# Token norms one projection earlier, and the first head pair's substitution handed out inside the second pair

## The chip, the cores and the metric

One core of one Trainium2 chip. The time is the device time of one execution in microseconds, the median of three runs. The engines are TensorE (PE, matmuls and transposes), VectorE (DVE), ScalarE (ACT), GpSimd (POOL) and SyncE (SP, which issues most DMAs). Each runs its own queue of instructions in order and waits on semaphores for the others.

## The reference

A decoder layer on 2048 tokens of width 1024, in float32: a gated DeltaNet mixer with 8 heads of 128, then a squared-ReLU MLP of width 4096, each behind an RMS norm and with a residual, and a last RMS norm.

```python
proj = h @ w_in                                   # q, k, v, gate z, and b, a
qkv = silu(causal_depthwise_conv(proj[..., :3 * DN_WIDTH], conv_w))   # 4 taps
...
lower = where(strict, einsum('bhnid,bhnjd->bhnij', k_beta, k) * decay, 0.0)
rhs = concatenate([v * beta, k_beta * exp(gc)])
sol = triangular_solve(lower + eye, rhs, lower=True, unit_diagonal=True)
...
x = x + gated_deltanet(rms_norm(x, norm_mix))
x = x + squared_relu_mlp(rms_norm(x, norm_mlp))
return rms_norm(x, norm_final)
```

The triangular matrix of each chunk of tokens is inverted: the 32x32 blocks on its diagonal by forward substitution, row by row, the rest from these blocks by matmuls.

## The kernel before

**Blocks and halves.** The tokens go in two blocks of 1024. Each block runs its mixer and then its MLP; the two mixers lie at about 0 to 740 and 1440 to 2200 us of the span. A mixer goes through two halves of 512 tokens (s = 0 and 1), and in each through the 8 heads in four pairs.

**A pair** has six projections, in the order k, k, q, q, v, v, counted by `n` from 1 to 6. Each is 24 matmuls of 128x512 (L117 to L119, 8 slices of the width, each as three products of high and low parts) into a PSUM bank `pj`, of which there are three. ACT copies it to `raw` (L303, L304; two buffers), DVE adds the other three taps (three L307), ACT takes a tanh (L310) and DVE finishes the SiLU (L311). After the third and fourth projection stand the key matrices (L428 on PE, L430 and L438 on DVE, with the decay factors `dt` of L413 and L415). In block 0's first half the weights come raw: POOL splits each into two parts (L90, L91) and SP keeps the result in DRAM; later they are read back.

**The substitution** of a pair is the generator `rows_of`: a transpose `pr` (L324), then 31 pairs of a multiply (L332) and a sum (L334) on DVE, in 24 steps. Its result `tt` is transposed at L344 (`tr`), and from there the inverse is built on PE and ACT (L364 to L391). This inverse, transposes of keys and values (L468), and the scores of queries and keys (L477) are the stages of the *previous* pair (`prepare2`), one stage behind each projection of the current pair. `wind_up` then runs the previous pair's two gate projections (L535, L536) and its chain over the chunks (L495 to L514, ending in the output `o`, L529), into which rows of the current pair's substitution are filled. For the first pair of a mixer there is no previous pair, and all its rows are handed out at once behind its projections.

**The norm of the other half.** In the first half (s = 0), each pair also norms one tile of 128 tokens of the second half: a DMA of the tile `xt`, the sum of squares on ACT (L180), a reciprocal root by DVE (L145, L130, L131, three L135 and L139), the scaled tile `xn` (L181), eight transposes on PE (two groups of four L186) and the split into two parts (L189 on ACT, L190 on DVE). The first pair computes the decay gates besides (`gg`, L263, which PE sums up at L268).

**What sets the order.** The program order gives priorities; a scheduler lists each engine's instructions from them once, and each queue then runs in that order whatever comes. `xt`, `xn` and `pr` share four buffers.

Of the kernel before, what the change touches and what calls it, by code (L numbers as in the profile page):

```python
# [7 lines left out]
F32 = mybir.dt.float32  # L8
# [8 lines left out]
P = 128  # L17
D = 1024
# [4 lines left out]
HB = 512  # L23
HT = HB // P
HP = 2
# [8 lines left out]
def tile_kernel(ctx: ExitStack, tc: tile.TileContext, x, w_in, w_out, w_up, w_down, n_mlp, n_fin, consts, out):  # L34
# [3 lines left out]
    pe, act, dve, pool, sp = nc.tensor, nc.scalar, nc.vector, nc.gpsimd, nc.sync  # L38
# [33 lines left out]
    for h in range(NH):  # L72
        s = cp.tile([P, P], F32, name=f"S{h}")
# [47 lines left out]
    def half_tiles():  # L121
        hh = hp.tile([P, KS, HB], F32R, name="hh", tag="hh")
        hl = hp.tile([P, KS, HB], F32R, name="hl", tag="hl")
        return hh, hl
# [52 lines left out]
    def norm_transpose(i, src, xn, wcol, hh, hl, tag):  # L177

        ssq = sm.tile([P, 1], F32, name="ssq", tag="ssq", bufs=3)
        act.activation(xn, src, AF.Square, accum_out=ssq)  # L180
        dve.tensor_scalar_mul(xn, src, rstd_of(ssq))  # L181
        ti = slice(i * P, (i + 1) * P)
        for k4 in range(0, KS, 4):
            ps = big(tag)
            for k in range(4):
                pe.transpose(ps[:, k * P:(k + 1) * P], xn[:, (k4 + k) * P:(k4 + k + 1) * P], ident)  # L186
            for k in range(4):
                src_, w = ps[:, k * P:(k + 1) * P], wcol[:, k4 + k:k4 + k + 1]
                act.activation(hh[:, k4 + k, ti], src_, AF.Copy, scale=w)  # L189
                dve.scalar_tensor_tensor(hl[:, k4 + k, ti], src_, w, hh[:, k4 + k, ti].bitcast(F32),  # L190
                                         op0=MULT, op1=SUB)
            yield
# [389 lines left out]
    def mixer(blk, hT):  # L582
        with tc.tile_pool(name="ap", bufs=2) as ap:
# [27 lines left out]
            def stages_of(sb, h, hT, qkv, gt, u):  # L611
                return prepare2(ap, sb, h, *qkv, gt, u, ub, t64)

            gt = None
            for s in range(2):
                sb = 2 * blk + s
                for h in range(0, NH, HP):
                    qkv, n = [], 0
                    stages = stages_of(*prev) if prev is not None else iter(())
                    next(stages, None)  # L620
                    if s == 0 and h == 0:
                        hT2 = half_tiles()
                    for part in (1, 0, 2):
                        d = ap.tile([P, HP * HB], F32, name=f"c{part}", tag=f"c{part}")
                        qkv.append(d)
                        for j in range(HP):
                            conv_part(ap, hT, part, h + j, d[:, j * HB:(j + 1) * HB], sb)
                            n += 1
                            next(stages, None)
                            if s == 0 and h == 0 and n <= 3:  # L630
                                if n == 1:
                                    gt = {}
                                    g_steps = gates(ap, sb, hT, gt)
                                next(g_steps)


                            if n == 3:
                                u = prepare(ap, sb, h, gt)
                                key_matrices(u, qkv[0], 0)
                            if n == 4:  # L640
                                key_matrices(u, qkv[0], 1)
                                key_norms(u)
                                rows_of = invert_diagonal(ap, u)
                                finish_ready()
                            if blk == 0 and s == 1 and n in (2, 5):
                                split_out(h // HP * 2 + n // 5)
                            if s == 0 and n == 1:
                                xt = wp.tile([P, D], F32, name="xt", tag="xt", bufs=4)
                                r0 = (sb + 1) * HB + h // HP * P
                                sp.dma_start(xt, x[r0:r0 + P, :])  # L650
                            if s == 0 and n == 2:
                                xt_steps = norm_transpose(
                                    h // HP, xt, wp.tile([P, D], F32, name="xn", tag="xt", bufs=4), nmix, *hT2, "po")
                            if s == 0 and n in (2, 4):
                                next(xt_steps)
                            if s == 0 and h == NH - HP and n >= 4:
                                if n == 4:
                                    gt2 = {}
                                    g_steps = gates(ap, sb + 1, hT2, gt2)
                                next(g_steps, None)  # L660
                    if prev is not None:
                        ready += wind_up(stages, rows_of, *prev)
                    for _ in rows_of:
                        pass
                    prev = sb, h, hT, (qkv[1], qkv[0], qkv[2]), gt, u
                if s == 0:
                    for _ in g_steps:
                        pass
                    hT, gt = hT2, gt2
# [224 lines left out]
```

## Time and profile before

| | us |
|---|---|
| median of 3 runs | 2877.57 (2872.32 to 2878.12) |
| the profiled execution | 2877.12 |
| its span | 2875.3 |
| PE busy in the span | 2751.3 |
| DVE busy in the span | 1563.4 |

The span runs from the first to the last instruction; 1.8 us of the profiled execution lie around it. The granted clock of TensorE is 0.98 of full speed over the whole span. In rows of the profile, "x4 [12.84 <-DVE xn L181]" says that four instructions ran, that the engine stood idle for 12.84 us before them, and that DVE's instruction of line 181, which writes `xn`, ended this idle time. In a row of a stretch the engines stand in the order PE, PEld (weight loads), DVE, ACT, POOL, each with its busy time and the number of instructions.

### The profile page before, as it was taken

The page shows a single profiled execution, that of the slowest core. Times are in us where ns is not written, and L with a number is a line of the kernel's source. Part 1 is how long each engine was busy: PE and PEld are TensorE (multiplying, and loading weights), DVE is VectorE, ACT ScalarE, POOL GpSimd, SP SyncE. Part 2 cuts the span into 40 slices and gives each one's busy share as a digit, 9 for nine tenths or more (in the row PEclk, how much of TensorE's full clock was granted, in tenths as well). Part 3 has the DMA queues.
Part 4 walks back from the last instruction along what each step waited for, and adds up shares of the span by engine and source line. Part 5 has one row for each costly group of instructions (what it writes and reads, how often), then busy time and mean ns, then how long its engine had stood idle before and what let it go on. Part 6 is the DMA issues. An engine that isn't in the chain of part 4 may idle for free.

```text
span 2875.3 us, 38577 instructions
## 1 busy us (share of the span) xinstructions
PE 2751.3 (96%) x14584; PEld 2278.5 (79%) x14584; DVE 1563.4 (54%) x3814; ACT 935.7 (33%) x2274; POOL 727.4 (25%) x646
## 2 busy tenths in 40 slices
PE   7788999999999999999999999999899999999998
PEld 6576778877788888888877888887787888888887
DVE  7887777763434333333388776777434333333335
ACT  4343444454221211211245555454423111112112
POOL 5443222210142332322311111111003322322321
PEclk9898999999999999999999999999999999999999
DMA  6544455556521211111144434444472111111111
GB/s 229 194 154 154 169 187 186 183 197 210 186 70 44 59 44 45 59 45 44 59 172 166 154 130 150 146 148 177 154 260 68 58 40 50 52 39 57 52 37 66
DMA packets 77482, 337.52 MB, mean 117 GB/s; under 512 B 8560, under 2 KB 8816, under 8 KB 55792
## 3 DMA queue, kind: packets, MB, share of 16 engines
q1 hardware_dynamic: 58480, 292.98, 30.3%
q10 hardware_dynamic: 18816, 42.08, 4.3%
q8 instruction: 114, 1.87, 0.3%
q14 instruction: 72, 0.59, 0.1%
HBM read 271.98 MB, written 63.05 MB: 117 GB/s over the span
## 4 chain that ended last, share of the span: by engine, by line
PE 79%; DVE 13%; ACT 5%; issue 2%; DMA 1%; POOL 1%; ACTq 0%; POOLq 0%; DVEq 0%; SPq 0%
PE pj L117 13%; PE pj L118 13%; PE pj L119 13%; PE kq L118 8%; PE kq L119 8%; PE kq L117 8%; DVE c L307 3%; DVE tmp L332 2%; PE kq L510 1%; DVE tt L334 1%; PE kq L504 1%; PE po L117 1%; PE po L119 1%; PE kq L495 1%; PE po L118 1%
## 5 line engine op out<-in xcount | busy, mean ns | idle before, releaser
L117 PE MATMUL pj<-hh,w 128*128 128x512 f32 x2048 | 819.6, 400 | 0.0
L118 PE MATMUL pj<-hh,w 128*128 128x512 f32 x2048 | 816.2, 399 | 0.0
L119 PE MATMUL pj<-hl,w 128*128 128x512 f32 x2048 | 814.1, 398 | 0.0
L119 PEld LDWEIGHTS pj<-hl,w 128*128 128x128 f32 x2048 | 389.6, 190 | 79.5 <-issue 0.6
L118 PEld LDWEIGHTS pj<-hh,w 128*128 128x128 f32 x2048 | 390.9, 191 | 76.7
L117 PEld LDWEIGHTS pj<-hh,w 128*128 128x128 f32 x2048 | 390.4, 191 | 76.8 <-issue 0.4
L739 ACT ACTIVATE r<-pj 128x512 f32<-128x512 f32 x128 | 76.6, 599 | 1066.0 <-PE pj L119 1066.0
L742 DVE TENSOR_TENSOR ul<-r,uh 128x512 fp32r<-128x512 f32 x128 | 146.8, 1147 | 485.6 <-ACT uh L741 485.6
L119 PE MATMUL kq<-dl,uh 128*128 128x512 f32 x992 | 386.9, 390 | 0.0
L118 PE MATMUL kq<-dh,ul 128*128 128x512 f32 x992 | 386.8, 390 | 0.0
L117 PE MATMUL kq<-dh,uh 128*128 128x512 f32 x992 | 386.7, 390 | 0.0
L782 DVE TENSOR_TENSOR x<-kq,x 128x512 f32<-128x512 f32 x256 | 176.6, 691 | 202.1 <-PE kq L119 199.4
L307 DVE SCALAR_TENSOR_TENSOR c<-raw,cst,c 128x512 f32<-128x512 f32 x288 | 246.4, 860 | 61.2 <-ACT c L304 58.6
L90 POOL TENSOR_SCALAR w<-wr 128x1024 fp32r<-128x1024 f32 x106 | 114.1, 1077 | 599.2 <-PE po L119 309.2
L782 DVE TENSOR_TENSOR x1h<-kq,x1h 128x512 f32<-128x512 f32 x256 | 176.5, 691 | 155.8 <-PE kq L119 155.6
L91 POOL TENSOR_TENSOR w<-wr,w 128x1024 fp32r<-128x1024 f32 x106 | 258.1, 2435 | 6.8
L90 POOL TENSOR_SCALAR dh<-wr 128x1024 fp32r<-128x1024 f32 x62 | 63.9, 1046 | 659.2 <-PE kq L118 626.4
L117 PEld LDWEIGHTS kq<-dh,uh 128*128 128x128 f32 x992 | 186.3, 188 | 40.3 <-DVE rm L145 1.4
L118 PEld LDWEIGHTS kq<-dh,ul 128*128 128x128 f32 x992 | 186.2, 188 | 39.4
L119 PEld LDWEIGHTS kq<-dl,uh 128*128 128x128 f32 x992 | 186.2, 188 | 38.8
L332 DVE TENSOR_TENSOR tmp<-tt,pr 128x2 f32<-128x2 f32 (+30 forms) x496 | 161.7, 326 | 10.3 <-POOL pr L325 0.5
L91 POOL TENSOR_TENSOR dl<-wr,dh 128x1024 fp32r<-128x1024 f32 x62 | 147.3, 2394 | 0.5
(313 smaller groups left out, 3432.7 us busy)
## 6 DMA issues: line engine op xcount, KB each, us to landing
w<-wi SPq DMA_DIRECT2D x96, 1024.0 KB, 4.9
wi<-w SPq DMA_DIRECT2D x32, 1024.0 KB, 4.8
wr<-in_w_up SPq DMA_DIRECT2D x64, 512.0 KB, 3.6
w<-wo SPq DMA_DIRECT2D x32, 1024.0 KB, 5.6
wr<-in_w_down SPq DMA_DIRECT2D x64, 512.0 KB, 3.5
wr<-in_w_in SPq DMA_DIRECT2D x32, 512.0 KB, 5.7
qe<-eg_d ACTq DMA_DIRECT2D x16, 512.0 KB, 3.8
o_d<-z2s ACTq DMA_DIRECT2D x32, 256.0 KB, 2.7
```

The lines of the kernel that those rows point to most:

```text
L90: pool.tensor_scalar(dst_h, src, 1.0, 0.0, op0=MULT, op1=ADD)
L91: pool.tensor_tensor(dst_l, src, dst_h.bitcast(F32), op=SUB)
L117: pe.matmul(ps, ah, bh, start=first and i == 0, stop=False)
L118: pe.matmul(ps, al, bh, start=False, stop=False)
L119: pe.matmul(ps, ah, bl, start=False, stop=last and i == n - 1)
L307: dve.scalar_tensor_tensor(dst, raw[:, k:k + HB], cw[:, 4 * f + k:4 * f + k + 1], dst, op0=MULT, op1=ADD)
L332: dve.tensor_tensor(tmp[:, 0:n, 0:i + 1], tt[:, 0:n, 0:i + 1], pr[:, i, 0:i + 1].unsqueeze(1).to_broadcast([P, n, i + 1]), op=MULT)
L334: dve.tensor_reduce(tt[:, 0:n, i], tmp[:, 0:n, 0:i + 1], axis=mybir.AxisListType.X, op=ADD)
L495: pe.matmul(ps[:, 0:P], u["k2"][:, c * P:(c + 1) * P], st[j], start=True, stop=True)
L739: act.activation(r, ps, AF.Relu)
L742: dve.tensor_tensor(ul[:, hs], r, uh[:, hs].bitcast(F32), op=SUB)
L782: dve.tensor_tensor(dst, ps, dst, op=ADD)
```

## The change

Two things change in both mixers, and all later lines of the program move on (L181 becomes L182, L186 L187, L344 L345, L364 L365, L468 L469).

1. The norm's generator yields once more, behind `xn`. The tile's DMA now stands ahead of the pair's first projection; the norm up to `xn` comes behind the first projection (n = 1), the two groups of transposes behind the second and the fourth. Before, the DMA stood behind the first projection, the norm and the first transposes behind the second.
2. The first pair's rows are no longer handed out at once. Behind the second pair's first projection come 12 of its steps, behind the second the other 12; the stages of the first pair start only then, and the last of them run in `wind_up` between the gate projections.

```diff
         dve.tensor_scalar_mul(xn, src, rstd_of(ssq))
+        yield
...
-                    next(stages, None)
-                    if s == 0 and h == 0:
-                        hT2 = half_tiles()
+                    late = s == 0 and h == HP
+                    if not late:
+                        next(stages, None)
+                    if s == 0:
+                        xt = wp.tile([P, D], F32, name="xt", tag="xt", bufs=4)
+                        r0 = (sb + 1) * HB + h // HP * P
+                        sp.dma_start(xt, x[r0:r0 + P, :])
+                        xt_steps = norm_transpose(
+                            h // HP, xt, wp.tile([P, D], F32, name="xn", tag="xt", bufs=4), nmix, *hT2, "po")
                     for part in (1, 0, 2):
...
                             n += 1
-                            next(stages, None)
+                            if s == 0 and n in (1, 2, 4):
+                                next(xt_steps)
+                            if late and n < 3:
+                                for _ in range(12 * n):
+                                    next(rows_of, None)
+                            if not late or n > 1:
+                                next(stages, None)
...
-                            if s == 0 and n in (2, 4):
-                                next(xt_steps)
...
-                    for _ in rows_of:
-                        pass
+                    if prev is not None:
+                        for _ in rows_of:
+                            pass
```

What this does to the queues shows at three places, all in block 0, first half. On TensorE, the start of the first pair's inverse (L364, now L365). Before, it stands in the middle of the second pair's last projection (w_1197, values), behind transposes of the first pair (c_606 its values, c_261 its keys):

```order
L117 MATMUL pj<-hh,w_1197 128x512
L118 MATMUL pj<-hh,w_1197 128x512
L468 MATMUL po<-cst,c_606 128x128 x4
L468 MATMUL po<-cst,c_261 128x128 x3
L364 MATMUL kq<-tcm,mt 32x32 x8
L468 MATMUL po<-cst,c_261 128x128
L119 MATMUL pj<-hl,w_1197 128x512
```

Now it stands in the projection behind that one (w_1206, the first gate), with the second pair's key products (c_692) next to it:

```order
L117 MATMUL pj<-hh,w_1206 128x512
L118 MATMUL pj<-hh,w_1206 128x512
L365 MATMUL kq<-tcm,mt 32x32 x8
L429 MATMUL kq<-c_692 128x128 x4
L119 MATMUL pj<-hl,w_1206 128x512
```

The inverse has moved behind 30 more dense matmuls, and the 16 transposes, eleven of which stood ahead of it, all follow it now.

On DVE, the second pair's scaled tile. Before, it stands among the later rows of the first pair's substitution, between two convolutions of the second pair's keys (c_774):

```order
L139 SCALAR_TENSOR_TENSOR rst<-rt,rst 128x1
L311 SCALAR_TENSOR_TENSOR c_774<-raw,c_774 128x512
L332 TENSOR_TENSOR tmp<-tt,pr 128x5x17
L181 TENSOR_SCALAR xn<-xt,rst 128x1024
L334 TENSOR_REDUCE tt<-tmp 128x5
L332 TENSOR_TENSOR tmp<-tt,pr 128x5x18
```

Now both pairs' scaled tiles (the second L181 below is the second pair's) stand around the very first convolution of the mixer (c_264, the first pair's keys):

```order
L181 TENSOR_SCALAR xn<-xt,rst 128x1024
L139 SCALAR_TENSOR_TENSOR rst<-rt,rst 128x1
L135 TENSOR_SCALAR rt<-rst,rh 128x1
L139 SCALAR_TENSOR_TENSOR rst<-rt,rst 128x1
L135 TENSOR_SCALAR rt<-rst,rh 128x1
L139 SCALAR_TENSOR_TENSOR rst<-rt,rst 128x1
L308 SCALAR_TENSOR_TENSOR c_264<-raw,cst,c_264 128x512
L181 TENSOR_SCALAR xn<-xt,rst 128x1024
L308 SCALAR_TENSOR_TENSOR c_264<-raw,cst,c_264 128x512 x2
```

The tile no longer waits for rows of the substitution.

On DVE, the end of the first pair's substitution. Before, it comes behind the first tap of the second pair's values (c_1110):

```order
L332 TENSOR_TENSOR tmp<-tt,pr 128x256
L307 SCALAR_TENSOR_TENSOR c_1110<-raw,cst,c_1110 128x512
L334 TENSOR_REDUCE tt<-tmp 128x8
L190 SCALAR_TENSOR_TENSOR hl<-po,cst,hh 128x128
L344 STREAM_TRANSPOSE tr<-tt 128x256
L307 SCALAR_TENSOR_TENSOR c_1110<-raw,cst,c_1110 128x512
```

Now the first head's values are done and two taps of the second head's as well (c_1089 holds both):

```order
L333 TENSOR_TENSOR tmp<-tt,pr 128x8x31
L312 SCALAR_TENSOR_TENSOR c_1089<-raw,c_1089 128x512
L335 TENSOR_REDUCE tt<-tmp 128x8
L333 TENSOR_TENSOR tmp<-tt,pr 128x256
L308 SCALAR_TENSOR_TENSOR c_1089<-raw,cst,c_1089 128x512
L335 TENSOR_REDUCE tt<-tmp 128x8
L308 SCALAR_TENSOR_TENSOR c_1089<-raw,cst,c_1089 128x512
L345 STREAM_TRANSPOSE tr<-tt 128x256
```

Five convolution instructions more stand ahead of the transpose. In block 1 the same places move likewise: the inverse stands behind 22 more dense matmuls, `xn` of the second pair among the gates' instructions ahead of `gg`, with three L307 (now L308) and an L311 of the queries ahead of `gg` too.

More of the change, by code (lines that the diff above doesn't have):

```diff
@@ L612, in stages_of @@
                 return prepare2(ap, sb, h, *qkv, gt, u, ub, t64)
-            gt = None
+            gt, hT2 = None, half_tiles()
             for s in range(2):
@@ L646, in mixer @@
                                 split_out(h // HP * 2 + n // 5)
[L647 to L653, printed above, removed]
-                            if s == 0 and n in (2, 4):
-                                next(xt_steps)
                             if s == 0 and h == NH - HP and n >= 4:
```

## The prediction

> **What bounds the kernel now.** I read the page first, then what TensorE waits for in the two mixers, then the stretches around those waits on TensorE and on DVE. From the page:
>
> ```profile
> span 2875.3 us, 38577 instructions
> PE 2751.3 (96%) x14584; PEld 2278.5 (79%) x14584; DVE 1563.4 (54%) x3814; ACT 935.7 (33%) x2274; POOL 727.4 (25%) x646
> PE 79%; DVE 13%; ACT 5%; issue 2%; DMA 1%; POOL 1%; ACTq 0%; POOLq 0%; DVEq 0%; SPq 0%
> ```
>
> TensorE is busy 96% of the span, so an edit that removes no matmul can win only its idle time and its slow time. DVE holds 13% of the chain though it is busy for half the span: somewhere DVE is the bound. The waits of TensorE, first in block 0's mixer (0 to 900 us), then in block 1's (1440 to 2200 us), with total, count and longest:
>
> ```profile
> PE po L186 <- ACT o L529: 12.9, 2, 7.7
> PE po L186 <- DVE xn L181: 12.8, 1, 12.8
> PE po L468 <- ACT vt L471: 7.4, 2, 5.2
> PE po L268 <- DVE gg L263: 4.5, 1, 4.5
> ...
> PE po L186 <- DVE xn L181: 5.8, 1, 5.8
> ```
>
> The change moves two things that stand here: the wait for the scaled token tile (L181, 12.8 and 5.8 us, one per block, both in the second head pair), and the place of the first pair's substitution. Around the larger wait TensorE reads:
>
> ```profile
> 93.24 1.11 PE L186 MATMUL po<-cst,xn 128*128 128x128 f32 x4 [12.84 <-DVE xn L181]
> ...
> 94.58 0.63 PE L119 MATMUL pj<-hl,w 128*128 128x512 f32 x1
> ...
> 98.84 0.53 PE L117 MATMUL pj<-hh,w 128*128 128x512 f32 x1
> ```
>
> From 94.58 to 98.84 lie ten dense matmuls, 0.43 us apart. What they take in a stretch where TensorE is never idle, and how the engines share the time around the wait, stands in the windows:
>
> ```profile
> 740.00:1440.00 700.00, 697.53 (x3089) 576.29 (x3089) 252.67 (x354) 131.91 (x223) 220.08 (x128) 1.00 0.19 60
> ...
> 57.00:122.30 65.30, 46.78 (x202) 37.89 (x200) 63.59 (x135) 26.32 (x62) 40.22 (x36) 0.87 0.56 198
> 122.30:150.00 27.70, 27.40 (x220) 22.77 (x220) 14.58 (x54) 16.35 (x38) 10.87 (x11) 0.86 0.43 147
> 150.00:187.00 37.00, 27.45 (x155) 23.69 (x155) 34.49 (x104) 10.61 (x37) 15.24 (x11) 0.92 0.43 147
> ```
>
> The columns are TensorE, weight loads, DVE, ACT, POOL, then the granted clock. In the MLP a matmul takes 697.53 / 3089 = 0.226 us, so the ten lost 4.26 - 2.26 = 2.0 us after the wait. From 57 to 122.3 us DVE is busy 63.59 of 65.30 us while TensorE has 18.5 us to spare: **here DVE is the bound, and the 12.84 us are only where that shows.** From 122.3 to 150 us it is TensorE (27.40 of 27.70), and from 150 DVE again. The border is the end of the first substitution:
>
> ```profile
> 120.71 1.11 PE L468 MATMUL po<-cst,c 128*128 128x128 f32 x4 [5.21 <-ACT vt L471]
> ...
> 122.33 0.43 DVE L344 STREAM_TRANSPOSE tr<-tt 128x256 f32<-128x256 f32 x1
> ...
> 123.50 1.06 PE L364 MATMUL kq<-tcm,mt 32*32 32x32 f32 x16
> ```
>
> L344 ends the substitution, and the inverse on TensorE starts with L364, 1.2 us behind.
>
> **The change, part by part.** Work is neither added nor removed; the sum is of places in the queues.
>
> *The second pair's norm, block 0.* It leaves the DVE stretch 57 to 122.3 us and goes in front of the first convolutions. What that stretch holds:
>
> ```profile
> L307 DVE SCALAR_TENSOR_TENSOR c<-raw,cst,c 128x512 f32<-128x512 f32 x22 | 27.0, 1228 | 0.2 <-ACT c L304 0.2
> L139 DVE SCALAR_TENSOR_TENSOR rst<-rt,rst 128x1 f32<-128x1 f32 x3 | 2.6, 877 | 0.0
> L135 DVE TENSOR_SCALAR rt<-rst,rh 128x1 f32<-128x1 f32 x3 | 0.8, 271 | 0.0
> L181 DVE TENSOR_SCALAR xn<-xt,rst 128x1024 f32<-128x1024 f32 x1 | 0.7, 747 | 0.0
> ...
> 85.88 2.33 DVE L139 SCALAR_TENSOR_TENSOR rst<-rt,rst 128x1 f32<-128x1 f32 x1
> ...
> 90.15 0.74 DVE L307 SCALAR_TENSOR_TENSOR c<-raw,cst,c 128x512 f32<-128x512 f32 x1
> ```
>
> The norm is 0.8 + 0.7 + 2.6 = 4.1 us, of which one L139 of 2.33 us was held by something that will hold another instruction instead: I take **-2.0** (bounds -4.1 and 0, the latter if the head has no room for it).
>
> *The substitution, block 0.* In the new order the last row and L344 stand behind five more convolution instructions of the pair's values: 5 x 0.74 = **+3.7**. The 22 L307 took 27.0 us instead of 22 x 0.74 = 16.3. The excess of 10.7 us lies beside POOL's splits of the weights:
>
> ```profile
> L91 POOL TENSOR_TENSOR w<-wr,w 128x1024 fp32r<-128x1024 f32 x8 | 20.3, 2539 | 0.2
> ...
> 94.35 2.88 POOL L91 TENSOR_TENSOR w<-wr,w 128x1024 fp32r<-128x1024 f32 x1
> ...
> 95.08 2.70 DVE L307 SCALAR_TENSOR_TENSOR c<-raw,cst,c 128x512 f32<-128x512 f32 x1
> ```
>
> Eight splits, 1.3 us of hold each. TensorE, no longer stopped at 80 us, frees weight buffers earlier, so one or two more splits (the gate projections') fall before L344: I take one, **+1.3** (0 to 2 x 2.0, the 2.70 row less 0.74). The Trainium skill ("SBUF — State Buffer", "Who interferes with whom") says that a DVE instruction with two SBUF inputs and a GpSimd instruction reading SBUF exclude each other for a whole instruction; the 2.70 us row beside the 2.88 us one agrees, and by it an extra split could cost its full 2.5 us, the sum then 1.2 us worse.
>
> *The gates, block 0.* DVE reaches gg some 1 us later (two more L307 and three more L430 ahead of it, but a shorter run of gate rows), while TensorE has 10 more dense matmuls in front of L268:
>
> ```profile
> 48.90 0.61 PE L268 MATMUL po<-gg,cst 128*128 128x32 f32 x2 [4.48 <-DVE gg L263]
> ...
> 51.02 0.63 PE L117 MATMUL pj<-hh,w 128*128 128x512 f32 x1
> ...
> 54.43 0.55 PE L119 MATMUL pj<-hl,w 128*128 128x512 f32 x1
> ...
> 57.30 0.29 DVE L430 SCALAR_TENSOR_TENSOR mt<-kq,cst 128x128 f32<-128x128 f32 x1 [3.58 <-PE kq L428]
> ```
>
> 10 x 0.226 = 2.3 less 1.0 is 1.3; eight steps from 51.02 to 54.43 took 3.4 instead of 1.8 us, and a shorter idle may save part of that. DVE waits for this at 57.30, so it counts: **-2.0** (-3 to +2).
>
> So L344 moves by -2.0 + 3.7 + 1.3 - 2.0 = **+1.0 us**, to about 123.3. TensorE, without the 12.84 us, reaches the inverse at about 107 us and waits there instead. What it has gained by then is order: 30 dense matmuls that stood behind L364 now stand ahead of it (6.8 us), and 11 of the 16 L468 transposes that stood ahead now follow (11 x 0.28 = 3.1 us by the 1.11 us row of four). From 122.3 to 150 us TensorE has 3.7 us less to do, and it is the bound there. Net in block 0: -3.7 + 1.0 = **-2.7 us** (-9 to +5).
>
> *Block 1.* The rows:
>
> ```profile
> 1543.45 1.12 PE L186 MATMUL po<-cst,xn 128*128 128x128 f32 x4 [5.80 <-DVE xn L181]
> ...
> 1565.48 0.69 PE L364 MATMUL kq<-tcm,mt 32*32 32x32 f32 x16 [0.20 <-ACT tcm L346]
> ...
> 1508.45 0.18 DVE L263 TENSOR_TENSOR gg<-gg,nexpa 128x32 f32<-128x32 f32 x1
> ...
> 1526.83 1.25 DVE L324 STREAM_TRANSPOSE pr<-xc 128x1024 f32<-128x1024 f32 x1 [0.99 <-ACT xc L322]
> ```
>
> The 5.80 us go, with about 0.6 us of slow matmuls behind them. TensorE comes to L364 with 22 more dense matmuls done (5.0 us), so 1.4 us sooner than now, when it waited 0.20 us: it will wait for the substitution. Against it, gg now follows three L307, an L311 and the norm's L181, about +4 us on 1508.45; the decay factors follow gg, the matrices them, and L324 them. DVE had about a microsecond of idle before L324, so I let the substitution start 2.5 us later, without the norm in its way (-2.0) but behind three more convolution instructions (+2.1 us): L344 comes +2.6. Net 2.6 - 5.0 = **-2.4 us** (-6.4 to +3).
>
> *The rest, at nothing.* The token tile's DMA stands in front of the pair's first weight on SP, and keep stores and loads of weights come in pairs: a load issued one split later. Its cover in block 0 is the wait at L364, over 12 us; without it a late weight costs up to a split, 2.5 us. The third and fourth pairs keep the order of their substitutions.
>
> Sum: 2877.1 (the profiled execution, 0.4 us below the median; its span is 1.8 us shorter) - 2.7 - 2.4 = 2872.0, or with a quicker inverse, since 30 matmuls fewer stand between its steps, about a microsecond less. I forecast **2871 us**.
>
> **The rivals.** *Both waits vanish whole.* If the DVE rows had room, 12.84 + 2.0 + 5.80 + 0.6 = 21.2 us would go, and the time be about 2856. For it: the two waits are the only ones for L181. Against it: DVE's 63.59 of 65.30 us. 0.12.
>
> *The waits only change their place.* TensorE stops at the inverse for as long as it stopped for the tile, and starts again at half pace, as it did after 12.84 us (ten steps, 2.0 us lost). L344 then comes 3 to 4 us later, and the 3.7 and 5.0 us of order are used up: 2875 to 2878. For it: DVE is the bound up to L344 and its work is the same. Against it: TensorE is the bound right behind. 0.30. The Trainium skill ("TensorE: Matmul & The Clock Gate", "What's actually happening") has the array at half rate after an idle window of about 3.4 us, until it has been busy about as long. The 12.84 us wait agrees. By that rule a wait of over 3.4 us at the inverse in block 1 costs the half rate that I left out, 1.7 us, and the sum would be 2873: it speaks against the change, which moves long waits rather than ends them.
>
> *Slower: the first substitution ends late.* If each of three further splits holds DVE for 2.0 us (the 2.70 row less 0.74) and the norm's room in front is not there, L344 in block 0 moves by 3.7 + 6.0 + 2.0 = 11.7 instead of 1.0 us; with 3.7 us of order against it, block 0 loses 8.0 us, and with block 1 at nothing the time is 2885. It decides from the point where L344 stands past about 126 us (122.33 + 3.7). For it: the 1228 ns mean of L307; against it: the eight splits there already cost only 1.3 us each. 0.18.
>
> **How the numbers follow.** My forecast has the remaining 0.40. What this kernel's measurement can tell from no change is about 0.2%, 5.8 us: 2871 is 6.6 us under the median, so just beyond. Faster by more than that: 0.31 of the forecast's 0.40 (2865 to 2876), the whole gain's 0.12, and 0.04 of the moved waits, where L344 comes earlier than they say; 0.47. Within: 0.09 of the forecast, 0.25 of the moved waits, 0.02 of the late substitution; 0.36. Slower: 0.16 and 0.01; 0.17. The range reaches from 2857, near the whole gain, to 2884, near the late substitution.
>
> **What would show it.** In the profile after: no wait for L181 in either mixer; the longest wait of the first mixer at the inverse's first matmul, for the copy behind L344, 12 to 18 us long; L344 within 2 us of 123 us; the second pair's transpose L324 (147.32 us now) some 3 us earlier. In block 1 gg near 1512 us and a wait of some 4 us at the inverse.
>
> ```profile
> 147.32 1.25 DVE L324 STREAM_TRANSPOSE pr<-xc 128x1024 f32<-128x1024 f32 x1 [1.87 <-ACT xc L322]
> ```
>
> Wrong would be made by an L344 past 126 us, by a wait for a weight's split in the second pair, or by a longer wait for L529 (12.9 us in two) that gives the 3.7 us back.

## The result, and the profile after

| | median us | runs | ratio to before (95%) |
|---|---|---|---|
| before | 2881.17 (2872.32 to 2889.08) | 20 | |
| changed | 2886.68 (2881.81 to 2890.97) | 20 | 1.0019 (1.0011 to 1.0027) |

Slower by 5.5 us (3.2 to 7.8), where 2871 was forecast, 6.6 us faster than the median of three runs that the forecast was counted from. That median, 2877.57, was 3.6 us under the 2881.17 of these twenty runs of the same kernel. The changed kernel's profiled execution took 2881.81 us, its fastest of the 20, over a span of 2880.0 us. From its page:

```profile
span 2880.0 us, 38585 instructions
PE 2759.5 (96%) x14584; PEld 2285.1 (79%) x14584; DVE 1563.9 (54%) x3814; ACT 936.0 (33%) x2274; POOL 727.3 (25%) x646
PE 75%; DVE 14%; ACT 5%; DMA 2%; issue 2%; POOL 2%; ACTq 0%; SPq 0%; POOLq 0%; DVEq 0%
```

The same 14584 matmuls are busy 8.2 us longer (2759.5 against 2751.3), and TensorE stands idle 3.5 us less (2880.0 - 2759.5 = 120.5 against 124.0). Between these two executions what was lost is not idle time: the matmuls ran slower. The waits of TensorE in block 0's mixer (0 to 900 us), with total, count and longest:

```profile
PE po L187 <- ACT o L530: 10.9, 2, 5.6
...
PE po L269 <- DVE cc L434: 6.1, 1, 6.1
...
PE kq L365 <- ACT tcm L347: 4.7, 2, 4.5
PE po L237 <- ACT kt L472: 4.6, 1, 4.6
PE pj L118 <- POOL w L91: 4.5, 2, 2.4
PE pj L117 <- POOL w L90: 4.4, 2, 2.8
```

and in block 1's (1440 to 2200 us):

```profile
PE kq L365 <- ACT tcm L347: 8.6, 3, 6.1
```

No wait for the scaled tile is left, as the change says. In its place stand four waits for POOL's splits of the weights (L90, L91), 4.5 us at the inverse (L365) and a longer wait at the gates' sum (L269, 6.1 us for 4.5). Where TensorE's time to the inverse went, row by row in block 0 and then at block 1's inverse:

```profile
81.23 0.50 PE L117 MATMUL pj<-hh,w 128*128 128x512 f32 x1 [1.61 <-POOL w L90]
84.11 0.79 PE L118 MATMUL pj<-hh,w 128*128 128x512 f32 x1 [2.38 <-POOL w L91]
...
112.33 0.51 PE L117 MATMUL pj<-hh,w 128*128 128x512 f32 x1 [2.75 <-POOL w L90]
114.94 0.79 PE L118 MATMUL pj<-hh,w 128*128 128x512 f32 x1 [2.10 <-POOL w L91]
115.53 0.63 PE L119 MATMUL pj<-hl,w 128*128 128x512 f32 x1
...
126.22 1.06 PE L365 MATMUL kq<-tcm,mt 32*32 32x32 f32 x16 [4.51 <-ACT tcm L347]
...
1569.60 1.05 PE L365 MATMUL kq<-tcm,mt 32*32 32x32 f32 x16 [6.13 <-ACT tcm L347]
```

Behind each pair of waits for the splits 14 dense matmuls start 0.43 us apart, half the pace of one every 0.226 us: TensorE reaches the inverse at 121.7 us, not 107. DVE's marks, and the stretch that answers to 57 to 122.3 us of before:

```profile
51.00 0.19 DVE L264 TENSOR_TENSOR gg<-gg,nexpa 128x32 f32<-128x32 f32 x1
...
125.05 0.44 DVE L345 STREAM_TRANSPOSE tr<-tt 128x256 f32<-128x256 f32 x1
...
143.06 1.25 DVE L325 STREAM_TRANSPOSE pr<-xc 128x1024 f32<-128x1024 f32 x1 [1.19 <-ACT xc L323]
```

```profile
57.00:125.05 68.05, 55.86 (x221) 44.15 (x219) 63.76 (x130) 24.82 (x57) 41.19 (x37) 0.90 0.57 209
```

DVE is still the bound to the end of the first substitution, with as much work as before (63.76 us against 63.59), and that end comes 2.7 us later (125.05 against 122.33). The second pair's transpose then comes 4.3 us earlier than before (143.06 against 147.32): up to there the forecast's order pays.

To see where a lead is won and lost I compare when TensorE starts the same dense matmul of w_in, counted from the start, as changed minus before: -2.7 us at 205 us, -1.9 at 272 and still at 292, +0.6 at 336, +1.2 at the end of block 0, and +4.7 at the end. Most of the lead goes at 292 to 336 us, in the fourth pair. The change moves the norm of a tile in that pair too, and with it the work around the second half's gates. There TensorE waits for a copy by ACT, before and changed:

```profile
316.44 1.06 PE L236 MATMUL po<-cst,bat 32*128 32x16 f32 x8 [2.83 <-ACT kt L471]
```

```profile
315.28 1.60 PE L237 MATMUL po<-cst,bat 32*128 32x16 f32 x8 [4.62 <-ACT kt L472]
```

From 292 to 331 us the changed kernel loses 2.6 us against before, and so does each of the three further profiles below that have its order there; before's own three further ones lose 0.0 to 1.1. The wait is 4.4 to 4.7 us in all eleven profiles whose block 0 has the moved norm, and 2.8 in all nine that have it as before. The experiments look for the rest: what block 0 loses against other executions of before, and block 1.

### The profile page after: what moved, and what is told of

The parts are those of the page before. It is cut to its first block, busy times and chain, and to the rows that moved or that the text cites. A ratio compares the mean times of both kernels' runs of the same rounds, so it can differ in the third digit from the quotient of the medians.

```text
span 2880.0 us, 38585 instructions
## 1 busy us (share of the span) xinstructions
PE 2759.5 (96%) x14584; PEld 2285.1 (79%) x14584; DVE 1563.9 (54%) x3814; ACT 936.0 (33%) x2274; POOL 727.3 (25%) x646
## 4 chain that ended last, share of the span: by engine, by line
PE 75%; DVE 14%; ACT 5%; DMA 2%; issue 2%; POOL 2%; ACTq 0%; SPq 0%; POOLq 0%; DVEq 0%
PE pj L118 13%; PE pj L117 13%; PE pj L119 13%; PE kq L119 8%; PE kq L118 8%; PE kq L117 8%; DVE c L308 3%; DVE tmp L333 2%; DVE tt L335 1%; PE kq L511 1%; PE kq L505 1%; PE po L117 1%; PE po L119 1%; PE po L118 1%; PE kq L496 1%
## 5 line engine op out<-in xcount | busy, mean ns | idle before, releaser
L117 PE MATMUL pj<-hh,w 128*128 128x512 f32 x2048 | 821.5, 401 | 4.6 <-POOL w L90 4.4
L117 PEld LDWEIGHTS pj<-hh,w 128*128 128x128 f32 x2048 | 391.0, 191 | 82.7 <-POOL w L90 5.0
L117 PE MATMUL kq<-dh,uh 128*128 128x512 f32 x992 | 386.6, 390 | 0.0
L308 DVE SCALAR_TENSOR_TENSOR c<-raw,cst,c 128x512 f32<-128x512 f32 x288 | 245.2, 857 | 61.4 <-ACT c L305 57.6
L91 POOL TENSOR_TENSOR w<-wr,w 128x1024 fp32r<-128x1024 f32 x106 | 258.9, 2443 | 7.0
L90 POOL TENSOR_SCALAR w<-wr 128x1024 fp32r<-128x1024 f32 x106 | 113.9, 1075 | 570.1 <-DMA wr<-in_w_up 210.2
L90 POOL TENSOR_SCALAR dh<-wr 128x1024 fp32r<-128x1024 f32 x62 | 63.9, 1047 | 659.0 <-PE kq L118 626.2
L117 PEld LDWEIGHTS kq<-dh,uh 128*128 128x128 f32 x992 | 186.2, 188 | 40.4 <-DVE rm L145 1.4
L91 POOL TENSOR_TENSOR dl<-wr,dh 128x1024 fp32r<-128x1024 f32 x62 | 147.3, 2394 | 0.5
```

The source lines that it names most:

```text
L90: pool.tensor_scalar(dst_h, src, 1.0, 0.0, op0=MULT, op1=ADD)
L91: pool.tensor_tensor(dst_l, src, dst_h.bitcast(F32), op=SUB)
L117: pe.matmul(ps, ah, bh, start=first and i == 0, stop=False)
L308: dve.scalar_tensor_tensor(dst, raw[:, k:k + HB], cw[:, 4 * f + k:4 * f + k + 1], dst, op0=MULT, op1=ADD)
```

## The experiments

Ratios are to runs of before on the same chip, taken beside each kernel's. Kernels without a ratio ran once.

**Each half of the change alone.** The norm alone undoes the second part of the change, the rows alone the first (both edits shortened):

```diff
-                            if late and n < 3:          # norm alone
-                                for _ in range(12 * n):
-                                    next(rows_of, None)
...
-                            if s == 0 and n in (1, 2, 4):   # rows alone: the norm's steps at n = 2 and 4 again
-                                next(xt_steps)
```

> Only the norm is moved; the first pair's rows are handed out at once as before. In its order gg (the gates' result on DVE) is late as in the changed kernel: 10 dense matmuls more ahead of L269 in each block. Gates theory (the norm step ahead of the gates makes gg, and with it the decay factors and the whole first substitution, late): gg near 1512 to 1515 us in block 1 (1508.45 before), L345 2 to 4 us later than before in both blocks, time 3 to 6 us above before. Weights theory (loads in pairs on SP make TensorE wait for POOL's splits): waits for a split's w of about 9 us in the first mixer again, time 3 to 6 us above before. Rows theory (handing out the rows later is what costs): no slower than before.

> Only the first pair's rows are handed out inside the second pair; norm and tile DMA as before, so gg and the second pair's xn stand where they stood. Gates theory: gg at 48.6 and 1508.4 us as before, waits for xn of about 13 and 6 us as before, time within 2 us of before. Rows theory: time 4 to 6 us above before, with the loss at the inverse L365. Weights theory: no waits for a split's w over 1 us, time as before.

Norm alone: 2874.26 us, 0.9977 (0.9965 to 0.9989): faster by 6.6 us, and by 12 us than both together. Rows alone: 2879.44 us, 0.9988 (0.9973 to 1.0003). Neither half is slow, so the sum of the parts' costs does not explain the whole; something between them does.

**The gates.** The changed order has `gg` 2.4 us later in block 0 and 6.4 us in block 1 (1.2 of them because the block starts later). Two kernels put it back in block 0, the first of them in block 1 too: the norm's step behind the gates' step, and the first pair's norm where it was (the second edit shortened).

```diff
-                            if s == 0 and n in (1, 2, 4):
-                                next(xt_steps)
...
                                 next(g_steps)
+                            if s == 0 and n in (1, 2, 4):
+                                next(xt_steps)
```

```diff
-                    if s == 0:
+                    if s == 0 and h:
                         xt = wp.tile([P, D], F32, name="xt", tag="xt", bufs=4)
...
+                            if s == 0 and h == 0 and n == 1:
+                                xt = wp.tile(...)           # DMA, norm and transposes of pair 1 as before
```

> The changed kernel with one swap: behind each projection the gates' step comes first and the norm's step second. gg is back at its old place (80 and 5072 dense matmuls ahead of it, as before), the inverse still stands 21 and 15 dense matmuls later than before, and xn of the second pair ahead of the rows that held it. Gates theory: gg at 48.6 and 1508.4 us, L345 within 1.5 us of 122.3 and 1564.3, no wait for xn, time 3 to 7 us below before. Weights theory: if the waits for a split's w stay near 9 us, time as the changed kernel's, 5 us above before. Rows theory: still 3 to 5 us above before.

> The changed kernel, but the first pair's tile is loaded and normed as before; only the second to fourth pairs' norm steps come early. gg is at its old place in block 0 (80 dense matmuls ahead of it) and still late in block 1 (5084 against 5072), and the second pair's xn stands at the head in block 0. Gates theory: block 0 gains 2 to 4 us against before by the end of its mixer, block 1 loses 2 to 4 us, sum within 2 us of before. Weights theory: the split's waits stay if SP still loads in pairs; time then 3 to 5 us above before with the loss in block 0. Rows theory: 3 to 5 us above before in both blocks.

Both are slower still: 2892.22 us, 1.0043 (1.0029 to 1.0057), and 2901.56 us, 1.0067 (1.0049 to 1.0085). The stretch around the inverse, 118 to 150 us, of the first and then of the second kernel:

```profile
118.00:150.00 32.00, 26.42 (x176) 21.18 (x176) 17.92 (x52) 11.63 (x24) 13.45 (x12) 0.55 0.45 164
```

```profile
118.00:150.00 32.00, 27.22 (x190) 22.77 (x191) 22.85 (x57) 15.32 (x37) 15.55 (x14) 0.61 0.41 148
```

The changed kernel has a clock of 0.85 there and before 0.84. So earlier gates win nothing back, and these two kernels lose at the inverse, where the clock shows it: TensorE waits 5.0 and 10.4 us there (changed: 4.5), and half rate lasts until 146 and 143 us (changed: 131), while it goes through the inverse's 32x32 and 64x64 matmuls with dense ones between them.

**One serial chain.** At 260 us DVE forms the reciprocal root of the second pair's output (L524, L130, L131 and three rounds of L137 to L139), twelve tiny instructions in a row; ACT scales the output with it (L530), and TensorE waits for that to get a `po` bank. In the changed kernel, DVE:

```profile
256.99 0.43 DVE L333 TENSOR_TENSOR tmp<-tt,pr 128x256 f32<-128x256 f32 x1
257.33 0.60 DVE L512 SCALAR_TENSOR_TENSOR S<-S,egt,kq 128x128 f32<-128x128 f32 x2
...
259.74 0.68 DVE L524 SCALAR_TENSOR_TENSOR nq<-ms,nq 128x8 f32<-128x8 f32 x1 [0.99 <-ACT o L521]
260.45 0.98 DVE L130 TENSOR_SCALAR rh<-nq 128x8 f32<-128x8 f32 x1
...
261.77 2.38 DVE L137 TENSOR_TENSOR rt<-rq 128x8 f32<-128x8 f32 x1
...
264.79 0.98 DVE L138 TENSOR_TENSOR rt<-rt,rh 128x8 f32<-128x8 f32 x1
...
266.00 2.20 DVE L137 TENSOR_TENSOR rt<-rq 128x8 f32<-128x8 f32 x1
...
268.44 0.17 DVE L139 SCALAR_TENSOR_TENSOR rq<-rt,rq 128x8 f32<-128x8 f32 x1
```

and POOL beside it, then TensorE:

```profile
258.00 2.39 POOL L463 TENSOR_TENSOR qe<-qe,c 128x1024 f32<-128x1024 f32 x1 [22.07 <-DMA qe<-eg_d]
260.36 1.04 POOL L90 TENSOR_SCALAR w<-wr 128x1024 fp32r<-128x1024 f32 x1
...
261.72 2.40 POOL L91 TENSOR_TENSOR w<-wr,w 128x1024 fp32r<-128x1024 f32 x1
...
264.71 1.04 POOL L90 TENSOR_SCALAR w<-wr 128x1024 fp32r<-128x1024 f32 x1 [0.46 <-PE pj L119]
265.84 2.34 POOL L91 TENSOR_TENSOR w<-wr,w 128x1024 fp32r<-128x1024 f32 x1
```

```profile
269.83 1.12 PE L187 MATMUL po<-cst,xn 128*128 128x128 f32 x4 [5.21 <-ACT o L530]
```

An instruction on 8 columns takes 0.17 us, and 2.38 when it starts beside a split: each such one ends just as POOL's does. I call that a hold. The chain takes 8.9 us, TensorE waits 5.21 us and starts again at half pace (1.12 us for four transposes).

Two ways to test this follow: take the chain off DVE, and profile the same orders again.

**The chain as one power on POOL**, everywhere in both kernels and in the norm alone:

```diff
-        rsqrt(rq, nq)
+        pool.tensor_tensor(rq, nq, nhalf[:, 0:NC], op=ALU.pow)
```

> The kernel before, with one edit: the reciprocal root rq of the chain's output (L130 to L139 on 128x8, 11 DVE instructions in a row) is one power on POOL (about 2.1 us by the rows of rk). Holds theory: in block 0 at the step from the third to the fourth pair these DVE instructions took 9.1 us beside POOL's splits in the kernel before and 8.9 us in the changed one, but 4.4 to 6.3 us in the two single edits; with them TensorE's 5.2 us wait for o (L529) and 11 us of half-rate matmuls behind it come or go, and that is the 7 to 8 us by which the single edits beat both. Then this kernel loses the wait there and its block 0 is 5 to 9 us shorter than before. Rival (the order of TensorE's queue decides, not the holds): block 0 within 2 us of before.

> The changed kernel with rq as a power on POOL. Holds theory: no wait for o over 2 us at the step from the third to the fourth pair in block 0, the half-rate stretch behind it gone, block 0 shorter than the changed kernel's by 5 to 9 us; time 4 to 9 us below the changed kernel, so 0 to 4 us below before. Rival (order): time within 2 us of the changed kernel. Block 1 has no splits, so both theories leave its 3.5 us loss.

> The norm alone, with rq as a power on POOL. Holds theory: the step from the third to the fourth pair was already free of the wait, so block 0 within 3 us of the norm alone (6.8 us under before); with the other pairs' chains shorter by 1 to 2 us each at most 4 us better. Rival (order): no statement, within 2 us of the norm alone.

All slower: 2898.67 us, 1.0058 (1.0041 to 1.0075) in before; 2913.46, 1.0099 (1.0075 to 1.0122) in the changed kernel; 2898.14, 1.0047 (1.0032 to 1.0062) in the norm alone. At the place itself it does what the theory of the holds says: in before, TensorE is 10.2 us ahead at 272 us and 8.6 at 336. From 420 us on, where POOL splits only one weight in 36 us and the chain on DVE takes 2.3 to 5.0 us, the edit only costs: 8 us behind at the end of block 0. So I confined it to the first half of block 0:

```diff
+        pool.tensor_tensor(rq, nq, nhalf[:, 0:NC], op=ALU.pow) if u["sb"] == 0 else rsqrt(rq, nq)
```

> The kernel before, with rq as a power on POOL in the first half of block 0 alone, where the splits run. In the run with it everywhere the chain's last copy there came 10.2 us sooner at the step from the third to the fourth pair, and 16 us were lost again in the three halves without splits. Holds theory: block 0 is 6 to 9 us shorter, block 1 as before, time 0.2 to 0.3% below before. Rival (the gain is given back in the second half whatever happens): time within 0.1% of before.

> The changed kernel, with rq as a power on POOL in the first half of block 0 alone. With it everywhere the marks behind the third pair came 4.5 to 4.9 us sooner than in the changed kernel. Holds theory: 4 to 6 us below the changed kernel, so within 2 us of before. Rival: no change against the changed kernel, 0.15 to 0.25% above before.

In before: 2879.43 us, 0.9989 (0.9979 to 0.9998), a gain of 3.2 us. In the changed kernel 2886.52 us, 1.0018 (1.0006 to 1.0029), none: there the edit also moved half rate to the first inverse (granted clock 0.60 at 118 to 150 us) and of the 5.0 us led at 272 us 2.4 were left at 336. For that kernel this pair of runs is no test.

**The same orders again.** One more profile of rows alone (its label names the power, but the kernel has no such edit), two more of before and two of the changed kernel:

> A second look at the rows alone, one profile and one time: by the holds theory and by its rival alike the same marks as the first look: block 0 about 8 us shorter than before, block 1 about 3.6 us longer. If the marks at the step from the third to the fourth pair differ by more than 3 us from the first look, these are chance of one execution and not of the order.

> The kernel before, a second profile. Two profiles of one kernel (the rows alone) agreed within 1.1 us at every mark of block 0 up to 235 us and were 6 us apart at its end and 10 us apart in the span. If that is the spread of any kernel, this profile agrees with the first within 1.5 us up to 235 us (L344 at 122.3, the first pair's chain done at 167.0, the second inverse at 190.3) and may differ by 3 to 6 us behind. If the first profile of before was an ordinary one, block 1 takes 797 us from its first projection to its MLP again (within 2 us).

> The changed kernel, a second profile. Same marks up to 235 us within 1.5 us (gg 51.0, L345 125.1, waits for a split's w of 8.9 us, L365's wait 4.5 us). In block 1, if the loss of 3.5 us against before is the order's: 800 to 801 us again, with waits of 6 and 2 us at the inverse and half-rate matmuls behind both. If it is chance: 797 to 799 us or over 802 us.

> The kernel before a third time, for its spread. Level with the two profiles of it within 1.6 us to 336 us in any theory. Block 1's mixer took 796.8 and 804.4 us in two profiles with the same order: if that is one choice of two behind the 2.4 us wait for L529, it takes one of these two again; if it drifts, something between.

> The changed kernel a third time. Its block 1 mixer took 800.2 and 800.6 us: the theory that its inverse always starts at half rate there gives 800 again; if 800 was chance as before's 797 and 804 were, it lies anywhere from 797 to 805. Level with its other profiles within 1.6 us to 336 us.

Their times: 2882.57 us (rows alone), 2890.77 and 2876.72 (before), 2886.50 and 2884.48 (changed). And, timed, the change in one block only (the switch `new` stands ahead of each edited line):

```diff
+                    new = blk == 0          # the other kernel: blk == 1
+                    late = new and s == 0 and h == HP
```

> The change in block 0's mixer alone; block 1's mixer keeps the order of before. The whole change measured +5.5 us (3.2 to 7.8). If the time lies in block 1 (inverse reached cold, 800 us for the mixer against 797), this one is within -2 to +2 us of before. If it lies in block 0 (more half rate behind the two waits of the second pair that moved), this one is +4 to +6. If each block has its half, +2 to +3. In the profile: at 336 us level with the changed kernel within 1.6 us under each theory.

> The change in block 1's mixer alone; block 0's keeps the order of before. If the time lies in block 1: +3 to +6 us, its mixer 800 us long with the wait at the inverse and half rate behind it. If it lies in block 0: 0 or -1. If each block has its half: +2 to +3. If the 5.5 us are chance of half-rate stretches far behind the change, this and the run with block 0 alone don't add up to it.

Block 0 alone: 2884.59 us, 1.0009 (0.9998 to 1.0020), +2.6 us. Block 1 alone: 2886.95 us, 1.0016 (1.0003 to 1.0029), +4.6 us. Block 1's part is clear of zero, block 0's is not by this run alone; together they make 7.2 us, in the bounds of the 5.5. The expectation that all profiles of one order stay level to 336 us fell in a telling way. The rows of before that was profiled a third time, at the same place, DVE and POOL, then TensorE:

```profile
259.58 2.67 DVE L332 TENSOR_TENSOR tmp<-tt,pr 128x256 f32<-128x256 f32 x1
...
263.11 0.12 DVE L523 SCALAR_TENSOR_TENSOR nq<-ms,nq 128x8 f32<-128x8 f32 x1
...
264.26 1.75 DVE L137 TENSOR_TENSOR rt<-rq 128x8 f32<-128x8 f32 x1
...
267.45 0.17 DVE L139 SCALAR_TENSOR_TENSOR rq<-rt,rq 128x8 f32<-128x8 f32 x1
```

```profile
259.57 2.40 POOL L462 TENSOR_TENSOR qe<-qe,c 128x1024 f32<-128x1024 f32 x1 [20.36 <-DMA qe<-eg_d]
```

```profile
268.84 0.66 PE L186 MATMUL po<-cst,xn 128*128 128x128 f32 x4 [0.40 <-ACT o L529]
```

and of before as first profiled, DVE and POOL:

```profile
258.73 0.61 DVE L511 SCALAR_TENSOR_TENSOR S<-S,egt,kq 128x128 f32<-128x128 f32 x2
...
259.69 0.43 DVE L332 TENSOR_TENSOR tmp<-tt,pr 128x256 f32<-128x256 f32 x1
```

```profile
259.78 2.58 POOL L462 TENSOR_TENSOR qe<-qe,c 128x1024 f32<-128x1024 f32 x1 [20.63 <-DMA qe<-eg_d]
```

One queue order, two outcomes, parted by when that last row of the third pair's substitution (L332) starts. If POOL's product `qe` starts 0.01 us *before* the row, the row is held (2.67 instead of 0.43 us), the chain starts 2 us later, behind `qe`, and the next split comes only when the chain is over: 4.51 us. If `qe` starts 0.09 us *after* it, the row goes free and the chain meets a hold for `qe` and for each split beside it, 9.10 us. All profiles of a kernel whose block 0 has one of these orders:

| block 0's order, profile | L332's start less qe's, us | chain, us | clock, 262 to 290 us | block 0's mixer, us |
|---|---|---|---|---|
| before, third | +0.01 | 4.51 | 1.00 | 720.0 |
| before, with the change in block 1 alone | +0.04 | 4.50 | 0.94 | 717.0 |
| rows alone | +0.05 | 4.50 | 0.94 | 715.6 |
| norm alone | +0.52 | 6.52 | 0.98 | 717.9 |
| rows alone, again | -0.02 | 9.10 | 0.88 | 721.8 |
| before | -0.09 | 9.10 | 0.76 | 723.7 |
| before, second | -0.25 | 9.10 | 0.76 | 729.8 |
| changed | -1.01 | 8.87 | 0.76 | 726.0 |
| changed, third | -1.13 | 8.91 | 0.76 | 724.7 |
| changed, in block 0 alone | -1.26 | 9.07 | 0.76 | 729.7 |
| changed, second | -1.33 | 9.08 | 0.76 | 729.7 |

The mixer is counted from its first dense matmul to its 593rd L117. Before tosses a coin of a tenth of a microsecond, rows alone too. **None of the four profiles with the changed order does: there the DVE queue has the row ahead of the chain's last update of the state (`S`, L512), where before has the update (L511) ahead of the row. The row starts a full microsecond before `qe`, and the serial chain is long each time.** In all eleven profiles `qe` starts 0.07 to 0.60 us behind the end of that update. Its second instruction starts 0.70 to 1.15 us ahead of the row in the seven profiles of before, rows alone and norm alone, and 0.60 us behind the row in all four with the changed order. So it takes both parts of the change to turn the two around, which fits that neither half is slow. The two kernels with the gates put back have the turned order too, and chains of 9.07 and 9.29 us. The four mixers with the shorter chains take 717.6 us on average, the seven with the long ones 726.5, and the groups do not overlap; of before's order alone, 717.0 and 720.0 stand against 723.7 and 729.8. The windows behind the table's fourth column, of before first profiled, before the third time, and changed:

```profile
262.00:290.00 28.00, 22.79 (x161) 17.89 (x162) 18.07 (x29) 14.64 (x39) 13.16 (x14) 0.76 0.39 141
```

```profile
262.00:290.00 28.00, 22.69 (x196) 18.03 (x196) 21.48 (x49) 18.04 (x45) 15.80 (x17) 1.00 0.56 188
```

```profile
262.00:290.00 28.00, 22.79 (x150) 17.83 (x149) 17.34 (x28) 14.42 (x38) 11.20 (x11) 0.76 0.44 154
```

TensorE is busy for the same 22.7 us of the 28, with 196 matmuls at full clock or 150 to 161 at 0.76.

**`qe` off POOL, in both kernels.** If the coin is block 0's cause, taking it away must bring the changed kernel down by more than before, and the two together:

```diff
-        (dve if c0 == NH * HT - NC and sb % 2 else pool).tensor_tensor(flat(qe), flat(qe), q2, op=MULT)
+        (dve if c0 == NH * HT - NC and sb % 2 or sb == 0 and c0 == 2 * NC else pool).tensor_tensor(...)
```

> The changed kernel, with the third pair's product qe (L463, block 0, first half) on DVE instead of POOL: the instruction beside which the serial chain of rq was held four times out of four profiles. DVE gets one instruction of about 1.1 us more there, and rows behind it change places. By the theory of the holds the chain from L524 to the last L139 takes 5 to 6 us instead of 8.9, the output of the second pair ends at 265 to 267 us instead of 270.4, and the median falls by 3 to 6 us, to 2881 to 2884. By the theory that the second half's half-rate stretches alone make the difference: the chain may be short, the median stays at 2885 to 2888.

> The same edit in the kernel before, where two of four profiles of the same order had the short chain already (4.5 us) and two the long one (9.1). By the theory of the holds: the short chain always, the median lower by half as much as in the changed kernel, 1.5 to 3 us (2879 to 2880.5); and the changed kernel with this edit lies within 3 us of this one, since the coin that the change turned is gone from both. By the rival: no difference to before, and the changed kernel's edit 5 us behind.

Changed: 2880.66 us, 0.9996 (0.9981 to 1.0011) of before. Before: 2878.95 us, 0.9989 (0.9976 to 1.0003). By the ratios the changed kernel comes down 6.6 us (from 1.0019; 3 to 6 were expected) and before 3.2, and 2.0 us are left between them, as the theory of the holds said and its rival did not. The changed kernel's intervals with and without the edit (0.9981 to 1.0011 and 1.0011 to 1.0027) just touch; those of the two kernels with it overlap widely. In the changed kernel's profile POOL, then the stretch:

```profile
258.64 2.05 POOL L90 TENSOR_SCALAR w<-wr 128x1024 fp32r<-128x1024 f32 x1 [22.33 <-PE pj L119]
260.78 2.38 POOL L91 TENSOR_TENSOR w<-wr,w 128x1024 fp32r<-128x1024 f32 x1
```

```profile
262.00:290.00 28.00, 25.76 (x190) 20.77 (x190) 19.97 (x46) 17.11 (x44) 13.42 (x16) 0.88 0.55 189
```

The chain itself did not go as expected: 6.9 us in the changed kernel and 7.9 in before rather than 5 to 6, since convolutions now stand between its instructions and one hold is left, and the output ends at 268.8 rather than 265 to 267 us. What came back is the clock, 0.88 for 0.76, and the fourth pair's transpose, 4.5 us earlier (301.1 against 305.6). The edit reorders rows around it, so it speaks for the place, and does not show that the hold is all of it.

## Why the prediction was wrong

**Block 0, net -2.7 us: right at 205 us, by luck.** There the changed kernel is 2.7 us ahead. But L345 came 2.7 us late instead of 1.0, so that 5.4 us must have been won behind it where 3.7 were summed: two misses that cancel. The gates gave a loss instead of -2.0: `gg` came 2.4 us later, not 1, TensorE waited 6.1 instead of 4.5 us ahead of its sum (L269), and the first pair's transpose started 3.3 us later. From there to L345 it took 0.6 us less than before, where norm, substitution and split were summed to +3.0; the convolutions in that stretch show why:

```profile
L308 DVE SCALAR_TENSOR_TENSOR c<-raw,cst,c 128x512 f32<-128x512 f32 x26 | 28.7, 1109 | 0.7 <-ACT c L305 0.7
```

Four more of them took 1.7 us more (28.7 against 27.0 us), so the excess beside the splits fell from 10.7 to 9.5 us rather than growing by 1.3.

**"TensorE reaches the inverse at about 107 us": 121.7.** Late weights were put at nothing, with the wait at the inverse as their cover. The four waits took 8.8 us and the 28 matmuls at half rate 28 x 0.2 = 5.6 more: 107 + 14.4 = 121.4 is nearly the 121.7. The cover held, with 4.51 us of it left instead of 12 to 18. This sign of failure came, and it was not what cost the time.

**"The third and fourth pairs keep the order of their substitutions", put at nothing: the step that failed.** It is not so in the queues. In the third pair DVE's last row now stands ahead of the state's last update, which `qe` follows; the row moved 2.7 us ahead (259.69 to 256.99) and `qe` only 1.8 (259.78 to 258.00), out of the coin's reach. The long serial chain, 5.2 to 5.4 us of wait for the output and the half rate behind it then come in all four profiles: 727.5 us for the mixer on average, against the 717.6 of the executions with a shorter chain. In the fourth pair the moved norm makes the wait for `kt` 4.6 us instead of 2.8, and 2.6 us are lost there. Timed alone, block 0 came out at +2.6 us (-0.6 to 5.8) instead of -2.7. A longer wait for L529 was named as a sign of failure, but the two profiled executions hide it: both have the long chain and wait 5.21 us for that output, and in all the wait for L529 is shorter, 10.9 us for 12.9. The chain's loss shows only against the executions of before that have the short one, the fourth pair's against both.

**Block 1, -2.4 us: +2.1 in the profiles, +4.6 (0.9 to 8.4) timed alone; a mis-sized term.** Counted from the same dense matmul at the block's start, as means over six profiles of each order, the inverse starts 1.5 us later (forecast 2.6, from L344), ends 4.4 later, and the first pair's output ends 2.1 later (the latest of before's six is 0.5 us ahead of the earliest of the changed); 2.2 remain at the third pair's. The wait at the inverse is 6.13 us where some 4 were said, and the inverse behind it takes 12.1 instead of 9.2 us. Before and changed, the 25 us from just ahead of its start:

```profile
1565.00:1590.00 25.00, 24.80 (x226) 21.08 (x225) 14.52 (x56) 15.53 (x37) 3.46 (x6) 1.00 0.34 119
```

```profile
1569.00:1594.00 25.00, 22.98 (x206) 19.23 (x207) 16.38 (x75) 15.41 (x39) 2.75 (x4) 0.88 0.17 64
```

A clock of 0.88 for 1.00. Of the 5.0 us of order only 2.3 are won back behind the inverse, and the inverse itself is 2.9 us longer; the half rate that the clock shows there was left out of the sum. That it makes up all of the difference no run shows. The rule of the Trainium skill ("TensorE: Matmul & The Clock Gate", "What's actually happening") that was set against the sum, half rate after an idle window of about 3.4 us, pointed the right way; the trace agrees, with 1.05 us for the 16 small matmuls behind the wait of 6.13 us (0.69 before).

**The inverse "quicker by a microsecond"** was not: 11.9 us in block 0, 12.0 before.

**The rivals.** *The waits only change their place* (0.30) was right in its mechanism: of TensorE's idle time in block 0's mixer, summed from the traces, 70.7 us of 73.6 are left, and it starts again at half pace. Its time, 2875 to 2878, was too low: it saw a wait moved within one pair and not what the moved work does to the next ones. *Both waits vanish whole* is out. *The late substitution* came near by its time (2885) and not by its cause: L345 at 125.05 stands below its 126.

Still open: half-rate stretches between 396 and 453 us come and go between executions of one order (two of before part there by 5 us behind equal marks), and the remaining difference with `qe` off POOL, 0.0007 of the time, is less than its interval.

## What to carry to other kernels

A lead won at one place is worth what the next meeting of two engines makes of it: before trusting one, compare the queue orders in the stretches behind it as well, look there for a serial chain of tiny instructions beside another engine's long ones, and ask who will start first now. Profile the same kernel several times before comparing two; where its executions fall in two groups, find the place where they part, for a change may choose between the groups rather than shift them. Of two edits that belong together by their idea, time each alone: here the norm alone, at 0.9977 of before, beats both kernels.

## What the runs showed of the hardware

- A DVE instruction on 128x8 that takes 0.17 us took 2.20 to 2.38 us beside a POOL split, and whether the chain was held turned on whether the row ahead of it started 0.01 us after POOL's `qe` or 0.02 us before it. The Trainium skill ("SBUF — State Buffer", "Who interferes with whom") has it that the order of issue decides who blocks; the table of eleven profiles agrees.
- Two short waits in a row brought half rate: 2.75 and 2.10 us with one matmul between them, then 14 dense matmuls 0.43 us apart. The Trainium skill ("TensorE: Matmul & The Clock Gate", "What's actually happening") has a free-running window of about 3.4 us; neither wait is that long, so here no single wait had to be.
- Behind a long wait ahead of the inverse's small matmuls the clock stayed low for long: 0.55 and 0.61 over 32 us, in the two kernels with the gates put back. Which of the matmuls kept it low no run shows.
